# A one-core hybrid decoder step in fp32: cache copies cut batch by batch, side sums and products on other engines, and some tiles at other addresses

## The chip, the cores and the metric

The kernel runs on one core of a Trainium2 chip. The time is device microseconds (us) of one launch, the median of the runs made. Five engines of the core work side by side, each through its own queue of instructions in order: PE (TensorE, matrix products), DVE (VectorE), ACT (ScalarE), POOL (GpSimd) and SP, which here issues DMA transfers only. ACT and POOL issue DMA transfers too.

## The reference

One layer of a decoder, run for a prompt of 1024 tokens and for 8 samples of 8 new tokens, together 1088 tokens of width 1024 (all fp32):

```python
x = x + 0.5 * swiglu(rmsnorm(x, ffn1_norm), ffn1_w_gu, ffn1_w_down)     # hidden width 2816
z = rmsnorm(x, mix_norm) @ w_in                                         # q, k, v, LRU, memory, gates
y_att = attend(q, k, v)            # 3 groups of 4 heads, windows 128, 512, 2048, dilations 1, 4, 16
y_rec = gelu(yr) * rglru(causal_conv(xr))                               # a gated recurrence
y_mem = memory_attention(qm)
x = x + (sigmoid(ga) * (y_att @ w_att_o) + sigmoid(gb) * (y_rec @ w_rec_o)
         + sigmoid(gc) * (y_mem @ w_mem_o)) @ w_out
x = x + 0.5 * swiglu(rmsnorm(x, ffn2_norm), ffn2_w_gu, ffn2_w_down)
y = rmsnorm(x, final_norm)
```

The samples read their keys and values from window caches (`cache_win_k0` to `cache_win_v2`: 8 samples, 128, 512 and 2048 rows of 256 floats), and the caches shifted by 8 rows are outputs of their own (`s_win_k0` to `s_win_v2`). Most of such an output is a plain copy from DRAM to DRAM.

## The kernel before, in words

**Stages.** Everything is held transposed (features in partitions, tokens along the free dimension). The stages follow each other: gate_up1 (the gate and up products of the first FFN, until about 590 us of the profile), down1 (its down product), the mixing part (memory heads, attention heads, then the recurrence in six tiles `lru_tile(0)` to `lru_tile(5)`, with 24 gate tiles strewn in where PE would wait), merge and out_proj, gate_up2 (from about 2030 us), down2 (from about 2530 us) and the final norm.

**One product is three.** `mac3` (L262 to L264) makes an fp32 product of a high and a low part of each operand, as three matmuls. The weights arrive in `wr` tiles by SP's DMAs; ACT rounds them to the high part (L167) and DVE subtracts for the low part (L168); these are the `ws` tiles.

**gate_up.** The hidden width is worked off in 22 pieces p of 128. The tokens lie in two halves tp of 544, and each half in two blocks of 272. The first PLAIN = 3 pieces are plain products (`plain`, L475). The others are "quads": `OPS` lists 7 products of Strassen's scheme in place of 8, whose weight operands are sums of weights, made by `combined` (L172 to L183) on POOL and DVE, and whose data operands `xo` are sums of blocks of x, made by `operands_of_blocks`, `norms_of_blocks` (squares by ACT, sums by L413), `gain_blocks` (L425 on POOL or DVE, L429 on ACT) and `sums_of_blocks` (L437, on DVE, with `put` at L373/L374). What is begun at the start of a stage as a generator (`begin1`, `begin2`) advances one step per `tick()`, and `tick()` is called between products. The last ALONE = 2 pieces are done for one half and then for the other, so that the down product's operand can be loaded meanwhile.

The evacuation (`swiglu`, L528 to L562) gathers the products of a quad in PSUM into `sl` and `uu`: DVE at L538 and L553, ACT at L543, POOL at L556 and L560 (the multiplication by the row factors `rb`). `gated_hidden` (L493) then has ACT's silu (L502), POOL's product (L505) and a DMA store from `sl` to the DRAM buffer `h_d` (L508), which is issued from ACT's queue. `sl` has three buffers: DVE writes a buffer again (L553) once its store has landed. The store's step in ticks is the tuple handed to `gated_hidden`.

**Cache copies.** `cache_copies` (L1545) makes a list of pieces, and `copies(n)` (L1560) issues the next n by DMAs in POOL's queue (L1563). gate_up1 calls `copies(1)` with each p but two, 20 times, gate_up2 `copies(2)` with each until none is left, and `copies(100)` stands at its end.

**The end of gate_up.** When the first half of the ALONE pieces is issued, `change()` closes pools and begins to load the hidden values back (`hr`, `hidden` at L565). In the kernel before, a loop ahead of it ticks until nothing is late.

**down.** `down_tile` (L641) sums the products over k in PSUM; the first sum goes to `x` by an ACT copy (L647), the later ones are added by DVE (L649). In down1 and down2 the squares of the finished x are summed on POOL or DVE (`sumsq`, L313 to L321), then `rstd` (L290 to L299) makes the factors, by a transposition on PE and a power on POOL.

**The sample attention.** `sample_scores` (L950) runs as a side job, a step every second tick: a DMA of a broadcast query into `qb` (L964), the product with the keys (L979, 48 in all: 24 on POOL, 24 on DVE) and the sum over features on DVE (L969). A step totals the product before, issues a load, and multiplies.

PE, ACT, DVE and POOL run in the order in which the code is written; SP's order is the framework's.

Of the kernel before, what the change touches and what calls it, by code (L numbers as in the profile page):

```python
# [53 lines left out]

FILL = (5, 4, 2)

# [4 lines left out]
class Kernel:  # L61
    def __init__(self, ctx, tc, ins, cst, outs):
        self.ctx, self.tc, self.nc = ctx, tc, tc.nc
        self.i, self.c, self.o = ins, cst, dict(zip(_OUTS, outs))
        self.n = 0
        self.ticks = 0
        self.first, self.side, self.due, self.hurry = [], [], [], False
        self.late = 0
        self.raws, self.ready, self.using, self.rest = [], [], 0, iter(())
# [47 lines left out]
    def make_plan(self):  # L117
        i = self.i
        col = lambda name, j: (name, i[name][j], 1024)

        def flat(name, off, n):
            return (name, i[name][off:off + 128 * n].rearrange("(p n) -> p n", p=128), n)

        def ffn(gu, dn):
            plan, off = [], 0
            for n, p in enumerate(TILES):
                plan += [(gu if n < PLAIN else "*" + gu, i[gu][q], 1024) for q in (p, KF + p)]
            for k, nk, w in DOWN:
                n = D if w == D else nk * w
                plan += [flat(dn, off + j * 128 * n, n) for j in range(nk * D // n)]  # L130
                off += 128 * nk * D
            return plan

        gates = [col("w_in", 34 + f) for f in range(24)]
        take = lambda n: [gates.pop(0) for _ in range(min(n, len(gates)))]
        mix = take(3) + [col("w_mem_kv", j) for j in range(8)] + [col("w_in", 30 + h) for h in range(4)]
        mix += take(FILL[0])
        for g, hp in UNITS:
            mix += [col("w_in", base + g * 2 + hp) for base in (12, 6, 0)]
        mix += take(FILL[1])  # L140
        for r in range(KR):
            mix += [col("w_in", 18 + r), col("w_in", 24 + r)] + take(FILL[2] - (r < 2))
        mix += take(24)
        merge = [("w_merge", i["w_merge"][f, u], 768) for f in range(KD) for u in range(2)] * 2
        outp = [col("w_out", f) for f in range(KD)] * 2
        self.plan = ffn("w_gu1", "w_dn1") + mix + merge + outp + ffn("w_gu2", "w_dn2")
# [59 lines left out]
    def make(self):  # L206

        for _ in self.rest:
            return
        if self.raws or self.plan:  # L210
            name, raw, n = self.raw()
# [96 lines left out]

    def norm_chunk(self, c, sq, wait):
        t0, n = CH[c]  # L310
        r = self.rstd(n, sq)
        self.later(wait, lambda: self.rows(self.rbc[:, t0:t0 + n], r, n))
# [119 lines left out]
    def sums_of_blocks(self, tp, xs, eng, rest=lambda: True):  # L432
# [7 lines left out]
        less(b22, b22, b11)  # L440
        yield
        self.put(tp, 6, b22)
        yield
# [10 lines left out]
    def plain(self, gu, p, order, pool):  # L454
# [3 lines left out]
        for tp in order:  # L458
            xo = self.xo[tp]
            sl, uu = (pool.tile([128, 2, TC], F32, name=self.uid(x), tag=x, bufs=n) for x, n in (("sl", 3), ("uu", 3)))  # L460
            for j, ms in enumerate(((1, 2), (0, 3))):
# [11 lines left out]
                def evac(j=j, rb=rb, both=both, sl=sl, uu=uu, tp=tp):  # L473
                    for t, ps in zip((sl, uu), both):
                        nc.vector.tensor_tensor(out=t[:, j], in0=ps[:, :TC], in1=rb, op=OP.mult)  # L475
                    if j:
                        self.gated_hidden(p, tp, sl, uu, (1, 2, 3))
                self.held.append(((tp, j), evac))
# [49 lines left out]
    def swiglu(self, p, tp, pool):  # L528
# [11 lines left out]
        def step(m, ps):  # L540
# [16 lines left out]
            if m == 3:  # L557
                sl = t["sl"]
                plus(sl[:, 1], ps, t["mu"])
                nc.gpsimd.tensor_tensor(out=sl[:, 1], in0=sl[:, 1], in1=rb[:, 1], op=OP.mult)  # L560
                self.gated_hidden(p, tp, sl, t["uu"])
        return step  # L562
# [26 lines left out]
    def gate_up(self, gu, first, pool, copies, misc, change):  # L589
# [15 lines left out]
        for tp in (first, second):  # L605
            for p in range(KF - ALONE, KF):
                self.quad(gu, p, (tp,), pool)
            if tp == first:
                while self.late:
                    self.tick()  # L610
                change()
# [336 lines left out]
    def sample_scores(self, g):  # L948
# [25 lines left out]
        for n in range(16):  # L974
# [3 lines left out]
            kk = kt[n][:, 0:1, :].to_broadcast([128, 4, 256]) if g == 0 else kt[n]  # L978
            (nc.vector if n % 2 else nc.gpsimd).tensor_tensor(out=prev, in0=prev, in1=kk, op=OP.mult)  # L979
            yield  # L980
# [565 lines left out]
    def cache_copies(self):  # L1546
        pieces = []
        for g, (W, _) in enumerate(GROUPS):
            for x in "kv":
                src, dst = (ap.rearrange("b w f -> b (w f)") for ap in (self.i[f"cache_{x}{g}"], self.o[f"s{x}{g}"]))  # L1550
                n = (W - 8) * 256
                nb, cut = ((8, 1), (2, 1), (1, 2))[g]
                for b in range(0, NB, nb):
# [12 lines left out]
def emit(K):  # L1566
# [9 lines left out]
    K.banks(ps0, "psum0", mm=8)  # L1576
    K.xo, K.plained, K.hurry, K.known, K.held = ({}, {}), False, True, set(), []
    of0, stage1 = left(low, "of0"), left(mid, "stage1")
# [30 lines left out]
    ops = [K.operands_of_blocks(tp, xs[tp], g, order) for tp in range(2)]  # L1609
    norms = [K.norms_of_blocks(tp, xs[tp], ev, eng) for tp, eng in enumerate((nc.vector, nc.gpsimd))]  # L1610
    for _ in range(2):
# [6 lines left out]
    def begin1():  # L1618
# [4 lines left out]
        yield from ops[1]  # L1623
        yield from norms[1]
        for _ in zip(K.gain_blocks(xs[0], g, nc.scalar), K.gain_blocks(xs[1], g, nc.gpsimd)):
            yield
        yield from K.sums_of_blocks(0, xs[0], nc.vector)
        spare.close()
# [35 lines left out]
    with ExitStack() as es:  # L1664
        K.tmps = right(es, "tmps1", 2)
        acc = {}

# [3 lines left out]
        def part(c, o):  # L1671
# [5 lines left out]
            K.split_x(c, o, xa, K.v["mix_norm"])  # L1677
            K.sumsq(o, xa, acc[c], n)
            if o % 4 == 3:
                nc.sync.dma_start(K.x_d[0][:, o - 3:o + 1, t0:t0 + n], K.x[:, o - 3:o + 1, t0:t0 + n])  # L1680
            if o == KD - 1:
                K.later(6 if c < 2 else 2, lambda: K.norm_chunk(c, acc[c], 5 if c < 2 else 2))
        K.down("w_dn1", pool, K.raw_tiles(pool), after)
# [12 lines left out]
    with ExitStack() as mix:  # L1696
# [42 lines left out]
        with ExitStack() as es:  # L1739
# [4 lines left out]
            for i in range(KR):  # L1744
                K.lru_tile(i)
                gate(FILL[2] - (i < 2))
            while K.due:
# [9 lines left out]
    K.banks(ps0, "psum5", mm=8)  # L1757
    K.xo, K.plained, K.known, K.held = ({}, {}), False, set(), []
    ev, of1, bb1, stage0 = left(low, "ev2"), left(low, "of1b"), left(low, "bb1"), left(low, "stage0b")
# [19 lines left out]
    def begin2():  # L1779
        yield from K.operands_of_blocks(0, xs[0], g, order, store(0))  # L1780
        yield from K.norms_of_blocks(0, xs[0], ev, nc.vector)
        for _ in zip(K.gain_blocks(xs[1], g, nc.scalar), K.gain_blocks(xs[0], g, nc.gpsimd)):
            yield
        yield from K.sums_of_blocks(1, xs[1], nc.vector)
        spare.close()
# [3 lines left out]
    def ready():  # L1789
        K.hurry = True  # L1790
        K.first += [K.operands_of_blocks(1, xs[1], g, order, store(1)), K.norms_of_blocks(1, xs[1], ev, nc.gpsimd)]
    K.out_proj(xs, ev, ready)
# [16 lines left out]
    with ExitStack() as es:  # L1809
        K.banks(es, "psum6", mm=6, t=2)  # L1810
        pool, K.tmps = left(es, "ffn2"), left(es, "tmps4", 2)
        K.x = pool.tile([128, KD, NT], F32, name="x2")
        acc = {}

# [5 lines left out]
        def square2(c, o):  # L1820
            t0, n = CH[c]
            xa = K.x[:, o, t0:t0 + n]
            if o < KD - 1 or c < 2:
                K.sumsq(o, xa, acc[c], n, nc.vector if c == 2 and o % 2 else None)
            else:
                last = K.tmp("ta")[:, :n]
                nc.scalar.activation(last, xa, AF.Square)
                r = K.rstd(n, acc[c], last)
            if c == 2:
# [6 lines left out]
        def after2(c, o):  # L1836
# [7 lines left out]
            if o == KD - 1:  # L1844
                K.later(5, lambda: K.norm_chunk(c, acc[c], 3))
                for j in range(4):
# [105 lines left out]
```

## Time and profile before

| | |
|---|---|
| median of 3 runs | 2820.39 us (2819.96 to 2821.05) |
| the profiled execution | 2824.31 us, its span 2822.5 us |
| PE busy | 2680.3 us (95%) |
| DVE busy | 1755.2 us (62%) |
| ACT busy | 910.8 us (32%) |
| POOL busy | 808.7 us (29%) |
| mean clock of PE | 0.977 of full |
| moved by DMA | 374.99 MB, 133 GB/s |

PE is nearly always at work, so the time is PE's work, plus the stretches in which PE waits, plus what it loses where the clock granted to it is below 1. A profile row such as "PE pg L262 <- DVE sl L553: 27.6, 5, 8.5" says that PE's instructions of line 262 that write `pg` waited in total 27.6 us, 5 times and 8.5 us at most, and that DVE's instruction of line 553 came last of what they waited for. A chain row such as "143.02 16.14 DMA h_d<-sl" says that from 143.02 us on the chain of work passes for 16.14 us through the store of `sl` to `h_d`.

### The profile page before, as it was taken

To read this page: it belongs to the slowest core of one execution; us is meant where nothing else is said; L and a number is where in the kernel's file an instruction comes from. 1 tells how busy PE (TensorE), PEld (TensorE's weight loads), DVE (VectorE), ACT (ScalarE), POOL (GpSimd) and SP (SyncE) were. 2 spreads that over 40 slices of the span, in tenths; PEclk is the share of its full clock that TensorE was granted. 3 is DMA by queue.
4 is the path that set the end of the run, shared out by engine and by line. 5 is a ranking of instruction groups with operands and counts; after the bars stand their busy time and mean duration, and the time that the engine had idled before them with its cause. 6 is when DMAs were issued, how large, how long until landed. Compare 5 with 4: busy or idle time off the path is not lost.

```text
span 2822.5 us, 46271 instructions
## 1 busy us (share of the span) xinstructions
PE 2680.3 (95%) x18076; PEld 2595.5 (92%) x18076; DVE 1755.2 (62%) x3018; ACT 910.8 (32%) x1747; POOL 808.7 (29%) x745
## 2 busy tenths in 40 slices
PE   7887899999999999999998999999999999989997
PEld 7887799999999889989987899999999999979997
DVE  5654656777785443466677656674567656576766
ACT  6321223321134322323334354432443223242112
POOL 3334455510021000021143321131235455453003
PEclk9998899999999999999999999999999999999998
DMA  4222334342225152375454431855426422243221
GB/s 166 92 88 97 115 130 151 137 173 92 93 96 187 65 163 87 117 242 163 145 183 144 154 114 66 278 173 185 167 102 226 171 105 83 73 138 120 90 78 64
DMA packets 181629, 374.99 MB, mean 133 GB/s; under 512 B 22345, under 2 KB 116745, under 8 KB 180737
## 3 DMA queue, kind: packets, MB, share of 16 engines
q1 hardware_dynamic: 166464, 303.85, 32.6%
q0 software_dynamic: 2272, 43.65, 4.3%
q10 hardware_dynamic: 12672, 24.52, 2.3%
q8 instruction: 142, 2.33, 0.3%
q14 instruction: 79, 0.64, 0.1%
HBM read 305.59 MB, written 113.16 MB: 148 GB/s over the span
## 4 chain that ended last, share of the span: by engine, by line
PE 73%; DVE 8%; DMA 7%; POOL 5%; issue 3%; ACT 3%; SPq 0%; DVEq 0%; ACTq 0%; POOLq 0%
PE pg L262 7%; PE pg L264 7%; PE pg L263 7%; PE z L262 7%; PE z L263 6%; PE z L264 6%; PE pd L262 6%; PE pd L263 6%; PE pd L264 6%; DMA h_d<-sl 4%; DVE ws L168 2%; PE po L264 2%; PE po L263 2%; PE po L262 2%; PE o L815 1%
## 5 line engine op out<-in xcount | busy, mean ns | idle before, releaser
L262 PE MATMUL pg<-xo,ws 128*128 128x272 f32 x2512 | 738.3, 294 | 72.1 <-DVE sl L553 27.6
L263 PE MATMUL pg<-xo,ws 128*128 128x272 f32 x2512 | 733.3, 292 | 0.0
L264 PE MATMUL pg<-xo,ws 128*128 128x272 f32 x2512 | 733.1, 292 | 0.1
L167 ACT ACTIVATE ws<-wr 128x512 fp32r<-128x512 f32 (+1 forms) x550 | 325.4, 613 | 914.7 <-PE pd L264 357.6
L168 DVE TENSOR_TENSOR ws<-wr,ws 128x512 fp32r<-128x512 f32 (+1 forms) x550 | 465.0, 869 | 151.8 <-ACT ws L167 151.4
L262 PEld LDWEIGHTS pg<-xo,ws 128*128 128x128 f32 x2512 | 483.0, 192 | 77.8 <-DVE sl L553 28.6
L262 PE MATMUL z<-xg,ws 128*128 128x368 f32 (+1 forms) x1392 | 478.1, 343 | 6.2 <-DVE ta L1394 6.2
L264 PEld LDWEIGHTS pg<-xo,ws 128*128 128x128 f32 x2512 | 483.1, 192 | 0.9 <-DVE ws L168 0.9
L263 PEld LDWEIGHTS pg<-xo,ws 128*128 128x128 f32 x2512 | 483.3, 192 | 0.0
L264 PE MATMUL z<-xg,ws 128*128 128x368 f32 (+1 forms) x1392 | 459.2, 330 | 0.0
L263 PE MATMUL z<-xg,ws 128*128 128x368 f32 (+1 forms) x1392 | 459.1, 330 | 0.0
L262 PE MATMUL pd<-h,ws 128*128 128x368 f32 (+1 forms) x1056 | 348.6, 330 | 10.4 <-ACT x L647 8.1
L263 PE MATMUL pd<-h,ws 128*128 128x368 f32 (+1 forms) x1056 | 346.5, 328 | 0.0
L264 PE MATMUL pd<-h,ws 128*128 128x368 f32 (+1 forms) x1056 | 345.9, 328 | 0.0
L649 DVE TENSOR_TENSOR x<-x,pd 128x368 f32<-128x368 f32 (+1 forms) x504 | 257.7, 529 | 134.4 <-PE pd L264 134.3
L262 PEld LDWEIGHTS z<-xg,ws 128*128 128x128 f32 x1392 | 264.3, 190 | 22.4 <-issue 13.1
L263 PEld LDWEIGHTS z<-xg,ws 128*128 128x128 f32 x1392 | 264.7, 190 | 1.3
L264 PEld LDWEIGHTS z<-xg,ws 128*128 128x128 f32 x1392 | 263.7, 189 | 0.0
L262 PEld LDWEIGHTS pd<-h,ws 128*128 128x128 f32 x1056 | 199.3, 189 | 11.3 <-ACT x L647 8.4
L263 PEld LDWEIGHTS pd<-h,ws 128*128 128x128 f32 x1056 | 199.4, 189 | 0.0
L264 PEld LDWEIGHTS pd<-h,ws 128*128 128x128 f32 x1056 | 199.3, 189 | 0.0
L183 POOL TENSOR_TENSOR wr<-wr,s 128x512 f32<-128x512 f32 x42 | 56.8, 1353 | 377.4 <-DVE ws L168 377.4
(295 smaller groups left out, 3745.2 us busy)
## 6 DMA issues: line engine op xcount, KB each, us to landing
wr<-in_w_gu_dram SPq DMA_DIRECT2D x96, 512.0 KB
wr<-in_w_in_dram SPq DMA_DIRECT2D x58, 512.0 KB
qb<-qs_d SPq DMA_DIRECT2D x48, 512.0 KB
h_d<-sl ACTq DMA_DIRECT2D x88, 272.0 KB
hr<-h_d SPq DMA_DIRECT2D x44, 544.0 KB
wr<-in_w_dn_dram SPq DMA_DIRECT2D x44, 512.0 KB
out_sk_dram<-in_cache_k_dram POOLq DMA_DIRECT2D x16, 1020.0 KB, 5.7
out_sv_dram<-in_cache_v_dram POOLq DMA_DIRECT2D x16, 1020.0 KB, 7.9
```

The source lines that it names most:

```text
L167: nc.scalar.activation(spl[:, 0, :n], src, AF.Copy)
L168: nc.vector.tensor_tensor(out=spl[:, 1, :n], in0=src, in1=spl[:, 0, :n].bitcast(F32), op=OP.subtract)
L183: eng.tensor_tensor(out=out, in0=x, in1=y, op=op)
L262: nc.tensor.matmul(out, wh, xh, start=start and i == 0, stop=False, **more)
L263: nc.tensor.matmul(out, wh, xl, start=False, stop=False, **more)
L264: nc.tensor.matmul(out, wl, xh, start=False, stop=i == n - 1, **more)
L649: nc.vector.tensor_tensor(out=xa, in0=xa, in1=ps[:, :n], op=OP.add)
L815: nc.tensor.matmul(po[:, e], pt[:, h, j * 128:(j + 1) * 128], z["vt"][:, kb[j], e], start=j == 0, stop=j == len(kb) - 1)
```

## The change

1. `cache_copies`: the pieces are cut from one sample each, with 16 rows as the outermost dimension (`nb = 1`), 1 piece a sample for group 0 (120 KB), 1 for group 1 (504 KB), 2 for group 2 (1020 KB). That makes 64 pieces in place of 42 (2 of 960 KB for group 0, 8 of 1008 KB for group 1, 32 of 1020 KB for group 2). The calls of `copies` are as before.
2. `FILL`: one gate tile more between the attention heads and the recurrence, one fewer after the third recurrence tile.
3. `make()` makes no combined weights before the norms of both halves are done (`normed`). The norms' additions of the second half are on DVE in place of POOL in both FFNs; the gains change places between ACT and POOL, and one of them runs beside the norms. `sums_of_blocks` has one step more.
4. `gated_hidden` of the plain pieces and of the ALONE pieces runs at other ticks; L560 of the ALONE pieces is on DVE; the loop ahead of `change()` is gone.
5. All 48 products of `sample_scores` are on POOL.
6. The last chunk of tokens in down1 and down2 has its sums of squares in two tiles, even o on POOL in the one and odd o on DVE in the other, which `rstd` adds up (in down1 all of them were on POOL in one tile; in down2 they alternated into one tile).
7. `x` of down2 stands in a pool of its own behind `tmps4` and `ffn2`, so that its address is another one.

```diff
-FILL = (5, 4, 2)
+FILL = (5, 5, (1, 1, 1, 2, 2, 2))
...
-            mix += [col("w_in", 18 + r), col("w_in", 24 + r)] + take(FILL[2] - (r < 2))
+            mix += [col("w_in", 18 + r), col("w_in", 24 + r)] + take(FILL[2][r])
...
-        if self.raws or self.plan:
+        if (self.raws or self.plan) and (self.normed or (self.raws or self.plan)[0][0][0] != "*"):
...
-    def norm_chunk(self, c, sq, wait):
+    def norm_chunk(self, c, wait, *sq):
         t0, n = CH[c]
-        r = self.rstd(n, sq)
+        r = self.rstd(n, *sq)
...
         less(b22, b22, b11)
         yield
+        yield
         self.put(tp, 6, b22)
...
-                        self.gated_hidden(p, tp, sl, uu, (1, 2, 3))
+                        self.gated_hidden(p, tp, sl, uu, (2, 3, 4))
...
-                nc.gpsimd.tensor_tensor(out=sl[:, 1], in0=sl[:, 1], in1=rb[:, 1], op=OP.mult)
-                self.gated_hidden(p, tp, sl, t["uu"])
+                (nc.gpsimd if p < KF - ALONE else nc.vector).tensor_tensor(out=sl[:, 1], in0=sl[:, 1], in1=rb[:, 1], op=OP.mult)
+                self.gated_hidden(p, tp, sl, t["uu"], (4, 5, 7) if p < KF - ALONE else (1, 3, 4))
...
             if tp == first:
-                while self.late:
-                    self.tick()
                 change()
...
-            (nc.vector if n % 2 else nc.gpsimd).tensor_tensor(out=prev, in0=prev, in1=kk, op=OP.mult)
+            nc.gpsimd.tensor_tensor(out=prev, in0=prev, in1=kk, op=OP.mult)
...
-                nb, cut = ((8, 1), (2, 1), (1, 2))[g]
+                nb, cut = 1, (1, 1, 2)[g]
...
-    norms = [K.norms_of_blocks(tp, xs[tp], ev, eng) for tp, eng in enumerate((nc.vector, nc.gpsimd))]
+    norms = [K.norms_of_blocks(tp, xs[tp], ev, eng) for tp, eng in enumerate((nc.vector, nc.vector))]
...
-        yield from norms[1]
-        for _ in zip(K.gain_blocks(xs[0], g, nc.scalar), K.gain_blocks(xs[1], g, nc.gpsimd)):
-            yield
+        for _ in zip(norms[1], K.gain_blocks(xs[0], g, nc.gpsimd)):
+            yield
+        K.normed = True
+        yield from K.gain_blocks(xs[1], g, nc.scalar)
...
-            K.sumsq(o, xa, acc[c], n)
+            if c == 2 and o % 2:
+                K.sumsq(o // 2, xa, odd, n, nc.vector)
+            else:
+                K.sumsq(o, xa, acc[c], n)
...
-        yield from K.norms_of_blocks(0, xs[0], ev, nc.vector)
-        for _ in zip(K.gain_blocks(xs[1], g, nc.scalar), K.gain_blocks(xs[0], g, nc.gpsimd)):
-            yield
+        for _ in zip(K.norms_of_blocks(0, xs[0], ev, nc.vector), K.gain_blocks(xs[1], g, nc.gpsimd)):
+            yield
+        K.normed = True
+        yield from K.gain_blocks(xs[0], g, nc.scalar)
...
-        K.first += [K.operands_of_blocks(1, xs[1], g, order, store(1)), K.norms_of_blocks(1, xs[1], ev, nc.gpsimd)]
+        K.first += [K.operands_of_blocks(1, xs[1], g, order, store(1)), K.norms_of_blocks(1, xs[1], ev, nc.vector)]
...
-        pool, K.tmps = left(es, "ffn2"), left(es, "tmps4", 2)
-        K.x = pool.tile([128, KD, NT], F32, name="x2")
-        acc = {}
+        K.tmps, pool, rest = left(es, "tmps4", 2), left(es, "ffn2"), left(es, "x2")
+        K.x = rest.tile([128, KD, NT], F32, name="x2")
+        acc, odd = {}, pool.tile([128, CMAX], F32, name="odd2", tag="odd", bufs=1)[:, :CH[2][1]]
...
-                K.sumsq(o, xa, acc[c], n, nc.vector if c == 2 and o % 2 else None)
+                if c == 2 and o % 2:
+                    K.sumsq(o // 2, xa, odd, n, nc.vector)
+                else:
+                    K.sumsq(o, xa, acc[c], n)
             else:
...
-                r = K.rstd(n, acc[c], last)
+                r = K.rstd(n, acc[c], odd, last)
```

**POOL's queue in gate_up1, around the first quad.** `wr` at L183 are combined weights, `uu` and `sl` the evacuation of the quad; the copies are L1563 before and L1562 after. Before:

```order
L1563 DMA out_sk_dram<-in_cache_k_dram 2x8x16128
L183 TENSOR_TENSOR wr_620<-wr_620,s_891 128x512
L183 TENSOR_TENSOR wr_900<-wr_898,wr_900 128x512
L183 TENSOR_TENSOR wr_898<-wr_898,s_1181 128x512
L556 TENSOR_TENSOR uu_1223<-uu_1223,rbc 128x544
```

And after:

```order
L1562 DMA out_sk_dram<-in_cache_k_dram 16x1920
L183 TENSOR_TENSOR wr_620<-wr_620,s_890 128x512
L183 TENSOR_TENSOR wr_899<-wr_897,wr_899 128x512
L183 TENSOR_TENSOR wr_897<-wr_897,s_1181 128x512
L557 TENSOR_TENSOR uu_1223<-uu_1223,rbc 128x544
```

The copy stands at the same place of the row; its shape was two outer rows of 8 by 16128 floats, and is 16 rows of 1920 floats.

**POOL's queue at the end of gate_up2.** The last two quads of the ALONE pieces, then the first residual additions of down2 (`x`, `xr`). Before:

```order
L556 TENSOR_TENSOR uu_25074<-uu_25074,rbc 128x544
L560 TENSOR_TENSOR sl_25111<-sl_25111,rbc 128x272
L505 TENSOR_TENSOR sl_25111<-sl_25111,uu_25074 128x544
L556 TENSOR_TENSOR uu_25206<-uu_25206,rbc 128x544
L560 TENSOR_TENSOR sl_25247<-sl_25247,rbc 128x272
L505 TENSOR_TENSOR sl_25247<-sl_25247,uu_25206 128x544
L1818 TENSOR_TENSOR x_25307<-x_25307,xr_25549 128x1088
```

And after:

```order
L557 TENSOR_TENSOR uu_25093<-uu_25093,rbc 128x544
L506 TENSOR_TENSOR sl_25131<-sl_25131,uu_25093 128x544
L557 TENSOR_TENSOR uu_25228<-uu_25228,rbc 128x544
L506 TENSOR_TENSOR sl_25268<-sl_25268,uu_25228 128x544
L1562 DMA out_sv_dram<-in_cache_v_dram 16x16320 x4
L1822 TENSOR_TENSOR x_25334<-x_25334,xr_25577 128x1088
```

The multiplication of `sl` by the row factors has left POOL, and four copies of 1020 KB have come in behind the last hidden product.

**DVE's queue where the recurrence begins.** `sst` totals a product of the sample attention, `qb` is the product itself, `xe` and `xc` are the convolution of the first recurrence tile. Before:

```order
L1322 SCALAR_TENSOR_TENSOR xc_13889<-xe_13888,vec,xc_13889 128x392 x3
L969 TENSOR_REDUCE sst_13518<-qb_13939 128x4x4
L979 TENSOR_TENSOR qb_13975<-qb_13975,kv_13937 128x1024
L168 TENSOR_TENSOR ws_14040<-wr_13598,ws_14040 128x512
L168 TENSOR_TENSOR ws_14043<-wr_13772,ws_14043 128x512
```

And after:

```order
L1321 SCALAR_TENSOR_TENSOR xc_14005<-xe_14004,vec,xc_14005 128x392 x3
L968 TENSOR_REDUCE sst_13520<-qb_14053 128x4x4
L168 TENSOR_TENSOR ws_14154<-wr_13774,ws_14154 128x512
L168 TENSOR_TENSOR ws_14157<-wr_13893,ws_14157 128x512
L1367 TENSOR_TENSOR lY_14009<-z_14141,rbc 128x352
```

DVE's product is gone from between the total and the next weight parts.

More of the change, by code (lines that the diff above doesn't have):

```diff
@@ L67, in __init__ @@
         self.first, self.side, self.due, self.hurry = [], [], [], False
-        self.late = 0
+        self.late, self.normed = 0, False
         self.raws, self.ready, self.using, self.rest = [], [], 0, iter(())
@@ L1576, in emit @@
     K.banks(ps0, "psum0", mm=8)
-    K.xo, K.plained, K.hurry, K.known, K.held = ({}, {}), False, True, set(), []
+    K.xo, K.plained, K.hurry, K.known, K.held, K.normed = ({}, {}), False, True, set(), [], False
     of0, stage1 = left(low, "of0"), left(mid, "stage1")
@@ L1665, in emit @@
         K.tmps = right(es, "tmps1", 2)
-        acc = {}
+        acc, odd = {}, K.tmps.tile([128, CMAX], F32, name="odd1", tag="odd", bufs=1)[:, :CH[2][1]]
         def after(c, o):
@@ L1681, in part @@
             if o == KD - 1:
-                K.later(6 if c < 2 else 2, lambda: K.norm_chunk(c, acc[c], 5 if c < 2 else 2))
+                K.later(6 if c < 2 else 2, lambda: K.norm_chunk(c, 5 if c < 2 else 2, acc[c], *([odd] if c == 2 else [])))
         K.down("w_dn1", pool, K.raw_tiles(pool), after)
@@ L1745, in emit @@
                 K.lru_tile(i)
-                gate(FILL[2] - (i < 2))
+                gate(FILL[2][i])
             while K.due:
@@ L1757, in emit @@
     K.banks(ps0, "psum5", mm=8)
-    K.xo, K.plained, K.known, K.held = ({}, {}), False, set(), []
+    K.xo, K.plained, K.known, K.held, K.normed = ({}, {}), False, set(), [], False
     ev, of1, bb1, stage0 = left(low, "ev2"), left(low, "of1b"), left(low, "bb1"), left(low, "stage0b")
@@ L1810, in emit @@
         K.banks(es, "psum6", mm=6, t=2)
-        pool, K.tmps = left(es, "ffn2"), left(es, "tmps4", 2)
-        K.x = pool.tile([128, KD, NT], F32, name="x2")
-        acc = {}
+        K.tmps, pool, rest = left(es, "tmps4", 2), left(es, "ffn2"), left(es, "x2")
+        K.x = rest.tile([128, KD, NT], F32, name="x2")
+        acc, odd = {}, pool.tile([128, CMAX], F32, name="odd2", tag="odd", bufs=1)[:, :CH[2][1]]
         def residual(o):
@@ L1844, in after2 @@
             if o == KD - 1:
-                K.later(5, lambda: K.norm_chunk(c, acc[c], 3))
+                K.later(5, lambda: K.norm_chunk(c, 3, acc[c]))
                 for j in range(4):
```

## The prediction

> **What bounds the kernel now.** I read the busy times first, then the stretches, then in each stretch who waited for whom. The page says that PE works 2680.3 us of the span, so the end is set by PE's work, by the holes in it and by the clock granted to it.
>
> ```profile
> PE 2680.3 (95%) x18076; PEld 2595.5 (92%) x18076; DVE 1755.2 (62%) x3018; ACT 910.8 (32%) x1747; POOL 808.7 (29%) x745
> ```
>
> The stretches below (columns: from and to, length, busy time and count of each engine, mean clock, DMA share, GB/s) are those with holes, but for the third, which has none.
>
> ```profile
> 0.00:113.00 113.00, 89.25 (x636) 87.61 (x637) 66.28 (x120) 54.85 (x111) 36.86 (x36) 0.92 0.34 128
> 113.00:327.00 214.00, 170.74 (x1239) 166.64 (x1238) 116.51 (x161) 50.30 (x88) 89.69 (x92) 0.90 0.27 96
> 327.00:548.00 221.00, 221.00 (x1750) 218.84 (x1750) 146.93 (x230) 67.60 (x120) 120.69 (x97) 1.00 0.40 138
> 548.00:592.00 44.00, 34.67 (x239) 33.06 (x238) 32.07 (x49) 17.62 (x29) 19.27 (x13) 0.96 0.76 288
> 840.00:862.00 22.00, 17.01 (x99) 16.16 (x98) 16.73 (x36) 12.85 (x26) 15.38 (x14) 0.92 0.49 158
> 1425.00:1525.00 100.00, 84.69 (x465) 78.45 (x464) 77.26 (x123) 43.71 (x59) 41.96 (x47) 0.91 0.47 147
> 2025.00:2100.00 75.00, 70.06 (x519) 69.04 (x519) 56.95 (x93) 38.97 (x76) 25.89 (x21) 0.95 0.46 163
> 2480.00:2545.00 65.00, 51.81 (x356) 50.48 (x354) 42.69 (x58) 26.35 (x47) 28.26 (x19) 0.89 0.39 133
> ```
>
> Two losses stand in such a row: length minus PE's busy time is the hole, and one minus the clock, times the length, is about what PE lost by running slower behind it. Row two has 43.3 us of holes and a clock of 0.90: by far the worst place, though it does the work of row three.
>
> **The copies (the largest term).** Between 113 and 327 us PE and DVE wait as follows, and the chain passes through the store of the hidden values once for each quad, six times, of which the first and the last:
>
> ```profile
> PE pg L262 <- DVE sl L553: 27.6, 5, 8.5
> ...
> DVE sl L553 <- DMA h_d<-sl: 85.4, 6, 16.3
> ...
> 143.02 16.14 DMA h_d<-sl
> ...
> 297.68 20.76 DMA h_d<-sl
> ```
>
> A store of 272 KB takes 16 to 21 us, DVE can't write `sl` again until then, and PE waits for DVE to empty PSUM. What lies in front of the stores is seen in the issues of the same stretch (count, KB each, median us to landing):
>
> ```profile
> out_sv_dram<-in_cache_v_dram POOLq DMA_DIRECT2D x4, 1008.0 KB, 24.0
> ...
> out_sk_dram<-in_cache_k_dram POOLq DMA_DIRECT2D x3, 1008.0 KB, 22.6
> ...
> out_sk_dram<-in_cache_k_dram POOLq DMA_DIRECT2D x1, 1020.0 KB, 5.3
> ```
>
> Nearly the same bytes land in 24.0 or 5.3 us, so it is the shape that decides: the slow pieces have 2 as their outermost dimension, the fast one 16, and while a slow one runs the stores land late. After the change every piece has 16 rows. In the third stretch there is such a piece of 16 rows for each p,
>
> ```profile
> out_sk_dram<-in_cache_k_dram POOLq DMA_DIRECT2D x10, 1020.0 KB, 5.3
> ```
>
> and PE has no hole at all.
>
> The price: row three does 1750 matmuls in 221 us, 0.1263 us each. The 1239 of row two would take 156.5 us at that pace instead of 214, so 57.5 us go. The bounds are 64.7 us (43.3 of holes and 0.10 × 214 = 21.4 of clock) and, if other waits come forward, about 45. I take **−57**.
>
> The Trainium skill, page "DMA: Bandwidth & Descriptors", section "Why a DMA increments its semaphore by 16 and not by 1", says that a transfer uses the largest number up to 16 of engines that divides its slowest dimension. By that rule the old pieces have 2 engines, the new ones 16, and the store is freed; the trace agrees in so far as 24.0 stands against 5.3 us.
>
> The rest of the copies moves: gate_up1 issues 16 pieces of 120 KB and 4 of 504 KB, gate_up2 two pieces with all of 20 p's in place of 11, and the last four (4.2 MB) go out at its end. In the first part of gate_up2, with two 1020-KB pieces for each p, the row is:
>
> ```profile
> 2100.00:2260.00 160.00, 160.00 (x1281) 159.96 (x1280) 99.46 (x157) 46.51 (x81) 78.12 (x67) 1.00 0.51 179
> ```
>
> No hole, clock 1.00, so I take nothing for the added p's. The four at the end meet the first loads of down2: by 4 × 5.3 us at most 21 us of queueing, covered by what down2 has already in its tiles; I take 0, the range has +5.
>
> **The end of gate_up2 (2480 to 2545).** Holes 13.2 us, clock 0.11 × 65 = 7.2 us.
>
> ```profile
> PE pd L262 <- ACT x L647: 8.1, 1, 8.1
> PE pg L262 <- DVE uu L538: 3.9, 2, 3.0
> ...
> ACT sl L502 <- POOL sl L560: 9.7, 2, 5.1
> ...
> ACT x L647 <- DMA h_d<-sl: 6.2, 1, 6.2
> ...
> 2530.76 7.08 DMA h_d<-sl
> ```
>
> The first copy to `x` waits for a store, since x2 lies where `sl` lay; with its own pool that wait is gone (the last row is the chain's: it goes through the store for 7.1 of PE's 8.1 us). What is late next is ACT's silu and POOL's product ahead of the store, which were through at 2530.76 us, about when PE began to wait; with L560 on DVE the silu, which waits for POOL in the third row, comes earlier. The removed loop took the 3.9 us with it: ACT, POOL and DVE were brought to a halt there. Of 20.4 us I take **−14**; ends −20 and −8 (the wait for `x` alone), since the load of `hr` still waits for the last stores.
>
> **The start (0 to 113).**
>
> ```profile
> PE pg L262 <- ACT ws L167: 19.1, 2, 11.6
> PE t L306 <- POOL rs L299: 2.9, 2, 2.3
> ...
> L413 POOL TENSOR_TENSOR acc<-acc,sq 128x272 f32<-128x272 f32 x14 | 10.7, 769 | 0.9
> ```
>
> The 11.6 us are the first load and stay. Of the 12.2 us of holes left and 9 of clock, POOL's additions (14 × 0.769 = 10.7 us) and the wait that follows go to DVE, and the first copy shrinks from 960 to 120 KB. DVE gets those 14 and keeps its long subtractions; the combined weights must wait for the norms, which can starve the first quads. **−7**; ends −14 and +3.
>
> **The end of gate_up1 (548 to 592).** The same loop and the same silu: holes 9.3, clock 1.8 us.
>
> ```profile
> PE pg L262 <- DVE uu L538: 6.5, 4, 3.1
> ...
> 566.77 10.60 DMA hr<-h_d
> ```
>
> The load of `hr` behind x's loads is untouched. **−4**; ends −11 and +2.
>
> **The end of down1.** POOL's chain of sums of the last chunk is halved by DVE's other tile. The row of 840 to 862 has 5.0 us of holes, of which
>
> ```profile
> PE t L294 <- POOL acc L321: 4.2, 1, 4.2
> ```
>
> DVE has 5.3 us free there. **−4** of 6.8 with the clock; ends −7 and −1.
>
> **The sample products.** A product is 1.217 us on DVE, 2.397 on POOL:
>
> ```profile
> L979 POOL TENSOR_TENSOR qb<-qb,kv x24: 2361/2397/2859, 1180.2 to 1482.6; 128x1024 f32<-128x1024 f32 x24
> L979 DVE TENSOR_TENSOR qb<-qb,kv x24: 1214/1217/1490, 1185.7 to 1491.7; 128x1024 f32<-128x1024 f32 x24
> ```
>
> DVE is freed of 24 × 1.217 = 29.2 us and POOL gets 57.5. Near 1246 us DVE stood at such a product, waiting for its load, with the attention's work queued behind it:
>
> ```profile
> DVE qb L979 <- DMA qb<-qs_d: 4.7, 1, 4.7
> ...
> PE s L786 <- DVE s L789: 1.7, 1, 1.7
> PE o L815 <- ACT pt L805: 1.1, 1, 1.1
> ```
>
> Now POOL waits there, and behind it stands little: **−3** (the two waits of PE, 2.8; ends −6 with the clock, and +2).
>
> At the start of the recurrence (1425 to 1525) DVE works 77 of 100 us, and PE waits:
>
> ```profile
> PE g L1333 <- issue: 7.5, 1, 7.5
> PE z L262 <- DVE ta L1394: 6.2, 2, 4.5
> ```
>
> There lie 15.3 us of holes and 9 of clock. Five products (6.1 us) leave DVE, and the gate tile that now comes ahead lets some steps of the side job end before the recurrence. Against it, in order of time, DVE's row of the chain without and with a product of POOL beside it, and that product:
>
> ```profile
> 1442.60 0.61 DVE xc L1322
> ...
> 1446.11 2.62 DVE xc L1322
> ...
> 1445.74 2.56 POOL L979 TENSOR_TENSOR qb<-qb,kv 128x1024 f32<-128x1024 f32 x1 [9.24 <-DMA qb<-qs_d]
> ```
>
> The convolution step took 0.61 us, and 2.62 where POOL's product ran from 1445.74 on: it ended 0.4 us after that did (1448.73 against 1448.30). I take **−6**, what leaves DVE; ends −16 and +19 (the rival below).
>
> The Trainium skill, page "SBUF — State Buffer", section "Who interferes with whom", says that a DVE instruction with two SBUF inputs and a GpSimd one that reads SBUF exclude each other for the whole instruction, so this part is bought dearer than it looks. The trace agrees: 2.62 against 0.61 us. By the rule alone, each of 24 products could hold DVE for up to 2.4 us, an estimate that would turn the −6 into a loss.
>
> **Merge to gate_up2 (2025 to 2100).** The same moves as at the start: holes 4.9, clock 3.8 us. **−3**; ends −8 and +5. The last norm's tiles I cost at nothing: their additions alternate between engines either way.
>
> **The sum.** −57 −14 −7 −4 −4 −3 −6 −3 = −98 us. From the profiled execution's 2824.31 us that is 2726.3; the median of the runs, 2820.39, lies 3.9 lower, so the forecast is **2722 us**.
>
> **Rivals.**
>
> *The products cost what they free (12%).* Each of the 24 moved products delays a DVE instruction by 2.62 − 0.61 = 2.0 us: 48 us against 29.2 freed, 19 us more for DVE in a part where it is nearly full. If all falls on PE, the −6 becomes +19: 2722 + 25 = 2747 us. For it speaks the row at 1446.11; against it, that half the products ran on POOL already and PE stood still for less than 3 us near 1246.
>
> *Only the stall of the stores goes (8%).* What else is moved comes out even: 2820.4 − 57 = 2763 us. For it, that DVE takes on additions where it is busy; against it, that the wait of `x` for a store is an address alone.
>
> *The change doesn't free the stores (5%).* They are as late behind pieces of 16 rows, or something else holds them: 2820.4 − 41 = 2779 us. Row three speaks against it.
>
> *Slower: bytes, not shape, delay the stores (2%).* Seven pieces in row two cost 57.5 us, 8.2 each. gate_up2 gets 18 more pieces; if each cost as much there, 148 us would be added: 2722 + 148 = 2870 us. It ends above the time before from 98 / 18 = 5.4 us a piece on. Against it: 160 us without a hole at two pieces a p.
>
> **Chances and range.** The forecast has 72%, its own range 2698 to 2745: the ends of the terms won't all fall together, so some 24 us to either side. With the products' rival and the one of the stall alone, 92% lie between 2698 and 2763; that is the range. About 0.2% (5.6 us) is what a measurement of this kernel can tell from no change: faster by more 97%, within it 1%, slower by more 2%.
>
> **What would show it.** Right: between 113 and 327 us no wait of DVE's L553 for `h_d`, quads of one pace through gate_up1, a clock near 1.00; no wait of ACT's first `x` copy for `h_d`; fewer than 10 us of holes around the end of gate_up2. Wrong: stores that land after 15 us in either gate_up (the copies); PE waiting for weights in the first quads (the start); longer waits of PE for DVE in 1180 to 1525 us, with the two-input rows of DVE stretched (the products); `hr` or weights late at the start of down2 (the four last copies). The forecast fails if gate_up1 loses less than 45 us.

## The result, and the profile after

The changed kernel takes 2746.96 us (median of 4 runs, 2746.11 to 2749.58) against 2820.18 us of the kernel before on the same chip: ratio 0.9743, 95% interval 0.9726 to 0.976, so about 73 us faster, where 98 were forecast. The profiled execution after took 2746.11 us (span 2744.3), and 78.2 us lie between it and the profiled one of before, which was itself 4 us above its median.

The stretches of the kernel after that answer to those of before (columns as there):

```profile
113.00:327.00 214.00, 214.00 (x1699) 212.08 (x1698) 133.83 (x226) 66.08 (x115) 119.29 (x119) 1.00 0.29 95
...
485.00:516.00 31.00, 25.80 (x188) 24.93 (x187) 27.35 (x39) 14.60 (x23) 12.06 (x8) 0.94 0.85 332
772.00:794.00 22.00, 17.86 (x104) 16.93 (x104) 17.56 (x39) 12.63 (x26) 10.39 (x10) 0.92 0.47 153
...
1380.00:1500.00 120.00, 104.62 (x606) 93.97 (x605) 94.31 (x180) 52.82 (x75) 55.52 (x66) 0.93 0.48 148
...
2420.00:2465.00 45.00, 39.87 (x288) 38.48 (x287) 36.50 (x51) 23.08 (x42) 20.68 (x15) 1.00 0.49 170
```

Between 113 and 327 us the holes are gone, the clock is full, and no wait of DVE's L554 for `h_d` is left. The end of gate_up1 (485 to 516), the end of down1 (772 to 794) and above all the start of the recurrence (1380 to 1500) still have holes. Who PE waits for in the last of these and at 1194 us, and how long the copies take to land in gate_up1:

```profile
PE t L1020 <- ACT ss L1012: 8.3, 1, 8.3
PE s L785 <- DVE s L788: 5.4, 1, 5.4
PE g L1332 <- DVE xc L1321: 3.5, 1, 3.5
...
out_sk_dram<-in_cache_k_dram POOLq DMA_DIRECT2D x4, 504.0 KB, 3.8
out_sk_dram<-in_cache_k_dram POOLq DMA_DIRECT2D x8, 120.0 KB, 3.2
```

Two waits for DVE and one for the sample softmax (behind DVE's L1011) are new in this size. The matrix products that bound the stages, read from the two traces (by their starts; the last product of down1 by its end), give the account of the time:

| stage | before, us | after, us | gain | forecast |
|---|---|---|---|---|
| gate_up1, until the first product of down1 | 582.9 | 515.7 | 67.2 | 68 (copies 57, start 7, end 4) |
| down1, until the end of its last product | 265.2 | 264.4 | 0.9 | 4 |
| mixing, until the last product of `z` | 944.5 | 947.6 | -3.1 | 9 (3 and 6) |
| merge, out_proj, until the first product of gate_up2 | 244.6 | 241.4 | 3.2 | 3 |
| gate_up2, until the first product of down2 | 486.9 | 484.3 | 2.6 | 14, with down2 |
| down2, until its last product | 276.3 | 269.4 | 6.9 | (see above) |

The row of the changed kernel's down products has the first boundary and, to 0.4 us, the last:

```profile
L262 PE MATMUL pd<-h,ws x1056: 317/330/508, 515.7 to 2722.4; 128*128 128x352 f32 x166, 128*128 128x368 f32 x10
```

So gate_up1 gained what was forecast, and the mixing part, which should have gained, lost. The loss is larger than this pair of traces shows: two kernels below whose mixing part is the one of before took 940.4 and 941.2 us for it (b_copies_new, b_g1_last). The experiments ask three things: was it the shape of the copies; what did the products on POOL cost; and what held the end of gate_up2 free.

### The profile page after: what moved, and what is told of

Same layout as the page of the kernel before. It is cut to its first block, busy times and chain, and to the rows that moved or that the text cites. A ratio compares the mean times of both kernels' runs of the same rounds, so it can differ in the third digit from the quotient of the medians.

```text
span 2744.3 us, 46291 instructions
## 1 busy us (share of the span) xinstructions
PE 2658.8 (97%) x18088; PEld 2578.8 (94%) x18088; DVE 1728.8 (63%) x3032; ACT 910.3 (33%) x1747; POOL 834.4 (30%) x751
## 3 DMA queue, kind: packets, MB, share of 16 engines
q1 hardware_dynamic: 166464, 303.85, 33.7%
## 4 chain that ended last, share of the span: by engine, by line
PE 83%; DVE 10%; ACT 2%; issue 2%; DMA 2%; POOL 1%; SPq 0%; DVEq 0%; ACTq 0%; POOLq 0%
PE pg L262 9%; PE pg L264 9%; PE pg L263 9%; PE z L262 7%; PE z L263 7%; PE z L264 7%; PE pd L262 6%; PE pd L263 6%; PE pd L264 6%; DVE ws L168 2%; PE po L264 2%; PE po L263 2%; PE po L262 2%; PE o L814 1%; PE wo L262 1%
## 5 line engine op out<-in xcount | busy, mean ns | idle before, releaser
L168 DVE TENSOR_TENSOR ws<-wr,ws 128x512 fp32r<-128x512 f32 (+1 forms) x550 | 439.4, 822 | 133.7 <-ACT ws L167 133.3
L262 PEld LDWEIGHTS pg<-xo,ws 128*128 128x128 f32 x2512 | 476.5, 190 | 21.3 <-DVE uu L539 12.8
L264 PEld LDWEIGHTS pg<-xo,ws 128*128 128x128 f32 x2512 | 476.4, 190 | 5.8 <-DVE ws L168 5.8
L263 PEld LDWEIGHTS pg<-xo,ws 128*128 128x128 f32 x2512 | 476.8, 190 | 0.0
L262 PEld LDWEIGHTS z<-xg,ws 128*128 128x128 f32 x1392 | 265.2, 191 | 15.7 <-issue 14.2
L978 POOL TENSOR_TENSOR qb<-qb,kv 128x1024 f32<-128x1024 f32 x48 | 116.2, 2424 | 198.0 <-DMA qb<-qs_d 146.6
```

Source lines behind the costliest of these rows:

```text
L168: nc.vector.tensor_tensor(out=spl[:, 1, :n], in0=src, in1=spl[:, 0, :n].bitcast(F32), op=OP.subtract)
L262: nc.tensor.matmul(out, wh, xh, start=start and i == 0, stop=False, **more)
L263: nc.tensor.matmul(out, wh, xl, start=False, stop=False, **more)
L264: nc.tensor.matmul(out, wl, xh, start=False, stop=i == n - 1, **more)
L978: nc.gpsimd.tensor_tensor(out=prev, in0=prev, in1=kk, op=OP.mult)
```

## The experiments

Ratios are to the kernel before on the same chip, with their 95% intervals; the medians of before there were 2822.8, 2821.4 and 2823.3 us in three groups of runs. A difference to the changed kernel is the difference of ratios times 2821 us. In traces of kernels whose gate_up1 is alike it ends between 514.6 and 519.3 us, so a difference of less than 5 us between two traces is not read there.

| kernel | median, us | ratio, interval | against the changed kernel |
|---|---|---|---|
| changed kernel | 2746.96 | 0.9743 (0.9726 to 0.976) | |
| a_copies_old | 2804.25 | 0.9933 (0.9919 to 0.9946) | +54 us |
| b_copies_new | 2774.57 | 0.9831 (0.9818 to 0.9845) | (48 us under before) |
| b_g1_last | 2800.15 | 0.9929 (0.9916 to 0.9943) | (20 us under before) |
| a_x2_old | 2768.78 | 0.9813 (0.9798 to 0.9829) | +20 us |
| a_flush | 2753.77 | 0.9759 (0.9745 to 0.9774) | +4.5 us |
| a_alternate | 2742.94 | 0.972 (0.9707 to 0.9734) | -6.5 us |
| a_dve_all | 2736.47 | 0.9697 (0.9684 to 0.9711) | -13 us |
| a_read | 2747.50 | 0.9738 (0.9722 to 0.9755) | -1.4 us |
| a_write | 2739.22 | 0.9708 (0.9692 to 0.9725) | -10 us |
| a_total_late | 2750.02 | 0.9749 (0.9731 to 0.9766) | +1.7 us |
| a_fill_old | 2747.84 | 0.9738 (0.9725 to 0.9752) | -1.4 us |
| a_dve_fill | 2736.39 | 0.97 (0.9683 to 0.9718) | -12 us |

**Was it the shape of the copies?** First the old pieces in the changed kernel:

```diff
-                nb, cut = 1, (1, 1, 2)[g]
+                nb, cut = ((8, 1), (2, 1), (1, 2))[g]
```

> The changed kernel with the cache copies cut as before (2, 8 and 32 pieces). Shape theory: pieces with 2 as outermost dimension hold up the stores of the hidden values, so the waits of DVE's L554 for h_d come back in the first third of gate_up1 and the time rises by 55 to 62 us, to about 2805 us. Rival, the stores were late for another reason that other parts of the change removed: less than 20 us, below 2767 us.

It takes 2804.25 us, 54 more, and DVE waits again as in the kernel before (between 113 and 327 us):

```profile
DVE sl L554 <- DMA h_d<-sl: 81.8, 6, 16.0
```

So the stall is the copies'. Then the new pieces alone in the kernel before (the same two lines the other way round):

> The kernel before with only the cache copies cut batch by batch. Shape theory: the whole stall goes, 55 to 60 us, to about 2763 us, and DVE's L553 doesn't wait for h_d between 113 and 327 us. Rival, that the copies need the other parts to pay: under 40 us, above 2780 us.

2774.57 us: 48 us, not 57, and short of what was expected. gate_up1 has them all: it ends at 519.5 us, 63.4 earlier than before, and PE works without a hole again:

```profile
113.00:327.00 214.00, 214.00 (x1697) 212.08 (x1697) 137.97 (x227) 66.94 (x117) 121.47 (x120) 1.00 0.28 96
```

But at the start of down2 the same kernel has (PE's wait, ACT's wait, and the chain between 2455 and 2490 us):

```profile
PE pd L262 <- ACT x L647: 18.9, 1, 18.9
...
ACT x L647 <- DMA h_d<-sl: 16.9, 1, 16.9
...
2465.76 17.83 DMA h_d<-sl
```

In the kernel before the same store took 7.08 us and PE's wait was 8.1. The four copies that now go out at the end of gate_up2 lie in front of it, and these 4.2 MB, issued within 2 us, land after 8.0 to 16.2 us although each has 16 rows. So the copies give some 11 us of their gain back there, as long as `x` lies where `sl` lay.

The last of this group keeps the pieces and the bytes of before and changes their order only, in the kernel before:

```diff
-        return pieces
+        return pieces[:2] + pieces[10:] + pieces[2:10]
```

> The kernel before with its own 42 pieces, only in another order: the eight pieces of 1008 KB (2 outer rows) last, the 32 of 1020 KB (16 rows) ahead of them, so that gate_up1 moves as many bytes as before. Shape theory: the stall leaves gate_up1 whole (some 57 us) and comes up in gate_up2 where the eight are issued, two by two in four p's, with some 20 to 40 us lost there: 2785 to 2805 us. Rival, that the bytes of a copy decide: gate_up1 stalls as before, and the time stays within 10 us of 2820 us.

2800.15 us, as the shape theory has it. Its gate_up1 and a part of gate_up2, what landed in each (the first row in gate_up1, the second in gate_up2), and the chain in gate_up2, first and last of four:

```profile
113.00:327.00 214.00, 214.00 (x1698) 212.08 (x1697) 137.40 (x225) 67.28 (x117) 118.71 (x120) 1.00 0.40 140
2100.00:2260.00 160.00, 137.64 (x1040) 136.12 (x1038) 84.81 (x119) 36.68 (x66) 66.33 (x57) 0.93 0.37 137
...
out_sk_dram<-in_cache_k_dram POOLq DMA_DIRECT2D x16, 1020.0 KB, 5.4
...
out_sk_dram<-in_cache_k_dram POOLq DMA_DIRECT2D x4, 1008.0 KB, 23.2
...
2147.64 19.47 DMA h_d<-sl
...
2242.61 19.52 DMA h_d<-sl
```

gate_up1 moves the same megabyte with each p as before (140 GB/s against 96) and has no hole; the stall has moved to gate_up2, to the four p's that issue the pieces of two outer rows, with a store of 19.5 us each. gate_up1 ends 57 us earlier than before (525.5 us), and gate_up2 takes 36 more (523.0 against 486.9). For this stall the bytes are no cause, the shape is.

**What held the end of gate_up2 free?** `x` of down2 back at its old place, the rest as changed:

```diff
-        K.tmps, pool, rest = left(es, "tmps4", 2), left(es, "ffn2"), left(es, "x2")
-        K.x = rest.tile([128, KD, NT], F32, name="x2")
+        pool, K.tmps = left(es, "ffn2"), left(es, "tmps4", 2)
+        K.x = pool.tile([128, KD, NT], F32, name="x2")
```

> The changed kernel with x of down2 back in the pool with ffn2, ahead of tmps4, where sl lay. Theory that the address keeps the end of gate_up2 free, and more so now that four copies go out there: ACT's first copy to x waits for the last stores again, behind 4 MB of copies, PE stands still 15 to 20 us at the start of down2 and loses some 8 us of clock behind it: 2768 to 2775 us. Rival, that other edits of the end (L560 on DVE, other ticks) already free it: within 5 us of 2747 us.

2768.78 us, 20 more, at the lower end of what was expected. It has the wait of the kernel with the new copies alone:

```profile
PE pd L262 <- ACT x L646: 18.3, 1, 18.3
...
ACT x L646 <- DMA h_d<-sl: 17.1, 1, 17.1
```

Then the loop ahead of `change()`:

```diff
             if tp == first:
+                while self.late:
+                    self.tick()
                 change()
```

> The changed kernel with the loop that ticks until nothing is late ahead of change again. Theory that the removed loop was worth what its waits showed, some 4 us in each FFN: 5 to 10 us slower, about 2754 us. Rival, that the waits of PE for DVE's L539 come from the order of the single quads and not from the loop: within 3 us of 2747 us.

2753.77 us: 4.5 us by the ratios, whose intervals overlap, where 5 to 10 were expected. PE's waits at the end of gate_up1 (480 to 525 us), with the loop and, in the second row, in the changed kernel without it:

```profile
PE pg L262 <- DVE uu L539: 7.1, 3, 3.0
```

```profile
PE pg L262 <- DVE uu L539: 6.6, 5, 3.1
```

They are nearly the same, so the waits that the forecast charged to the loop belong to the order of the single quads, as the rival said. Something does go with the loop, but little: gate_up2 takes 486.6 us with it, and 483.1 to 484.4 in the kernels that have the changed one's gate_up2.

**What did the products cost?** Alternating again, and all on DVE:

```diff
-            nc.gpsimd.tensor_tensor(out=prev, in0=prev, in1=kk, op=OP.mult)
+            (nc.vector if n % 2 else nc.gpsimd).tensor_tensor(out=prev, in0=prev, in1=kk, op=OP.mult)   # a_alternate
+            nc.vector.tensor_tensor(out=prev, in0=prev, in1=kk, op=OP.mult)                             # a_dve_all
```

> The changed kernel with the sample products alternating between POOL and DVE again. Theory that the all-POOL products cost the mixing part what was forecast as gain (DVE's total L968 now waits for POOL's product, 34 us in all): 6 to 14 us faster, about 2737 us, and the waits of L968 for POOL mostly gone. Rival, that the gate tile moved ahead of the recurrence or the attention's own order is what costs: within 3 us of 2747 us.

> The changed kernel with all 48 sample products on DVE. If the wait of the total for POOL's slow product is the cost, the load's latency stays and DVE waits at the product instead: about 2747 us, no better than alternating. If the cost is that POOL's product blocks DVE's two-input instructions, none is blocked now: faster than the alternating version, below 2737 us. If DVE's own load decides, 29 us more of DVE work over the alternating version: slower than 2750 us.

Alternating is 6.5 us faster by the ratios, but the intervals overlap, and its profiled execution, the slowest of its four, isn't faster; the waits of L968 for POOL's product fall to 3.7 us in it. All on DVE is 13 us faster, clear of the interval: the fastest version but for one that equals it. The groups of DVE between 1100 and 1440 us, in the changed kernel (total of a product, low parts of the weights, convolution):

```profile
L968 DVE TENSOR_REDUCE sst<-qb 128x16 f32<-128x1024 f32 x48 | 58.3, 1215 | 33.7 <-POOL qb L978 33.7
L168 DVE TENSOR_TENSOR ws<-wr,ws 128x512 fp32r<-128x512 f32 x40 | 32.9, 863 | 1.3 <-ACT ws L167 1.2
L1321 DVE SCALAR_TENSOR_TENSOR xc<-xe,vec,xc 128x352 f32<-128x352 f32 (+2 forms) x10 | 10.0, 1000 | 0.4
```

And with all products on DVE:

```profile
L978 DVE TENSOR_TENSOR qb<-qb,kv 128x1024 f32<-128x1024 f32 x48 | 59.3, 1236 | 11.4 <-DMA qb<-qs_d 11.0
L968 DVE TENSOR_REDUCE sst<-qb 128x16 f32<-128x1024 f32 x48 | 58.1, 1211 | 0.0
L168 DVE TENSOR_TENSOR ws<-wr,ws 128x512 fp32r<-128x512 f32 x40 | 25.7, 683 | 1.0 <-ACT ws L167 0.9
L1321 DVE SCALAR_TENSOR_TENSOR xc<-xe,vec,xc 128x352 f32<-128x352 f32 (+2 forms) x18 | 10.9, 604 | 0.6
```

Two things differ: DVE's total waits 33.7 us for POOL's product, and the instructions with two inputs take longer beside it (L168 863 ns against 683, L1321 1000 against 604; the total, with one input, is the same). Three kernels are to tell the two apart. In the first all products are on DVE and POOL does an idle product beside each, whose result nobody waits for; in the second POOL does fills in its place, which write only (in both a copy of one column makes POOL wait for DVE's product, and the keys have two buffers in place of three):

```diff
+            nc.gpsimd.tensor_copy(scr[:, 0, 0:1], prev[:, 0, 0:1])                          # both
+            nc.gpsimd.tensor_tensor(out=scr, in0=scr, in1=prev, op=OP.mult)                 # a_read
+            for _ in range(3):                                                              # a_write
+                nc.gpsimd.memset(scr, 0.0)
```

> The changed kernel with all sample products on DVE, and beside each of them a product of the same size on POOL that reads the query tile and a scratch tile and whose result nobody uses or waits for (the keys have two buffers in place of three, to make room). Theory that POOL's reading blocks DVE's two-input instructions: the 10 us that all-DVE won are lost again, 2744 to 2752 us, and the mean of L168 between 1100 and 1440 us rises from 0.68 to about 0.86 us. Rival, that the wait of the total for POOL's slow product was the cost: within 4 us of 2737 us, L168 at 0.7 us.

> The same with three fills of the scratch tile on POOL in place of the idle product, about as long, which write and don't read. If reading is what blocks: within 4 us of 2737 us, L168 near 0.7 us. If any work on POOL there delays (its own queue, or writing too): 2744 us or more.

```profile
L168 DVE TENSOR_TENSOR ws<-wr,ws 128x512 fp32r<-128x512 f32 x40 | 30.5, 804 | 0.2
...
L982 POOL TENSOR_TENSOR scr<-scr,qb 128x1024 f32<-128x1024 f32 x48 | 121.5, 2531 | 3.8
```

```profile
L168 DVE TENSOR_TENSOR ws<-wr,ws 128x512 fp32r<-128x512 f32 x40 | 25.7, 683 | 0.9 <-ACT ws L167 0.8
...
L983 POOL MEMSET scr<- 128x1024 f32 x144 | 137.5, 955 | 8.4
```

With the idle product (the first fence) the time is 2747.50 us, as slow as the changed kernel, and L168 takes 804 ns; with more POOL time spent in fills (the second) it is 2739.22 us and L168 takes 683 ns, as with POOL free. The load of the next query does have to wait until the idle product has read the tile, but that is not the cause: DVE waits 9.9 us in all for these loads in a_read, 8.5 in a_write and 11.0 in a_dve_all. The difference lies in the mixing part (bounds as in the table of the stages):

| | changed kernel | a_alternate | a_dve_all | a_read | a_write | a_total_late |
|---|---|---|---|---|---|---|
| mixing, us | 947.6 | 946.6 | 936.8 | 946.7 | 940.0 | 951.0 |

PE's wait for the convolution in a_read, and a step of it in the chain, which took 0.46 to 0.48 us with POOL free and ends here 0.2 us after POOL's idle product does:

```profile
PE g L1336 <- DVE xc L1325: 5.7, 3, 2.0
...
1388.01 2.54 DVE xc L1322
```

The third kernel leaves the products on POOL and totals each one step later, so that DVE should wait less:

```diff
-            if n:
-                total(n - 1, prev)
-            prev, cur = cur, fetch(n + 1)
+            if n > 1:
+                total(n - 2, two)
+            two, prev, cur = prev, cur, fetch(n + 1)
```

> The changed kernel, all products on POOL, with the total of a product one step later (three query tiles, two key tiles), so that DVE need not wait for a product that has just begun. Wait theory: the 34 us of waits of L968 shrink to a few and the time falls to about 2737 us. Theory that POOL's reading blocks DVE: the waits shrink too, but the time stays within 4 us of 2747 us, L168 at 0.86 us.

```profile
L968 DVE TENSOR_REDUCE sst<-qb 128x16 f32<-128x1024 f32 x48 | 58.0, 1212 | 11.1 <-POOL qb L978 11.1
L168 DVE TENSOR_TENSOR ws<-wr,ws 128x512 fp32r<-128x512 f32 x40 | 37.9, 986 | 7.1 <-ACT ws L167 7.0
```

The waits of the total fall from 33.7 to 11.1 us and the time doesn't: 2750.02 us. But this does not part the two causes. L168 rises from 863 to 986 ns meanwhile, and one of the waits that are left, of 7.7 us, lies in PE's way. In the changed kernel too the hole at 1194 us comes by such a wait: DVE's total stands behind a query's load and POOL's product, and the attention's scores (L788) behind the total. The chain there, in the changed kernel, and PE's wait for the scores that is left in a_total_late:

```profile
1187.33 5.20 DMA qb<-qs_d
...
1192.69 2.37 POOL qb L978
...
1196.22 2.59 DVE ws L168 x2
```

```profile
PE s L785 <- DVE s L788: 4.1, 1, 4.1
```

So a_read and a_write show that POOL's reading beside DVE is enough to make the mixing part as slow as in the changed kernel, with no wait for a product. In the changed kernel itself both are at work, and how its loss is shared between them stays open.

**The gate tile.** `FILL` as before, in the changed kernel and in the one with all products on DVE:

```diff
-FILL = (5, 5, (1, 1, 1, 2, 2, 2))
+FILL = (5, 4, (1, 1, 2, 2, 2, 2))
```

> The changed kernel with FILL as before, so that the recurrence begins one gate tile earlier. Theory of the forecast, that the tile ahead lets steps of the side job end before the recurrence: 3 to 8 us slower, about 2752 us. Rival, that the gate tile only moves work and the wait for the sample softmax stands there either way: within 3 us of 2747 us, or faster.

> The changed kernel with all sample products on DVE and FILL as before: the gate tile was worth nothing with POOL's products, so within 4 us of 2737 us. If DVE, fuller now, decides where the recurrence begins, the tile ahead of it is worth some 5 us: about 2742 us.

2747.84 and 2736.39 us: nothing either way. With the old FILL PE stands still where it did in the kernel before (between 1360 and 1500 us), with the new one for the sample softmax (8.3 us in the changed kernel, 8.4 with all products on DVE, so that wait is not the products'):

```profile
PE z L262 <- DVE ta L1393: 6.1, 2, 3.4
PE g L1332 <- issue: 5.5, 1, 5.5
```

## Why the prediction was right, and where its sum was off

The time lies within the range, 25 us above the forecast and 2 us above the forecast's own range (2698 to 2745), to which 72% were given. 5 us of the 25 are the profiled execution of before, which stood 4 us above its median where that of after stands 1 us below. The rest by the steps:

- *The copies*, -57: right in mechanism, and nearly in size. a_copies_old is 54 us slower, and b_g1_last shows that shape alone moves the stall. The rival that bytes decide falls with it. gate_up1 gained 67 of the forecast 68 us, of which the new pieces alone bring 63.4 (b_copies_new), 3.8 of these by the smaller first copy (below): some 60 where 57 were put down. That "the old pieces have 2 engines" fits the eight of 1008 KB only: the two of 960 KB have 8 as outermost dimension, and landed in 8.6 and 7.6 us.
- *The four last copies*, taken at nothing: nearly right in the changed kernel (down2 takes 269.4 us, and 267.4 in a_copies_old, which has none of them there), but only because `x` has its own place. b_copies_new shows the price without it, a hole of 18.9 us in place of 8.1. "Covered by what down2 has already" was not the cover; the address was.
- *The end of gate_up2*, -14: 9.6 measured. The wait of `x` went as the step says, and a_x2_old prices it at 20 us in the kernel as changed, more than was put down, since the copies lie there now. The 3.9 us laid to the loop did not go with it: PE still waits 4.0 us for DVE's L539 between 2420 and 2465 us.
- *The start and the end of gate_up1*, -7 and -4: some 8 us in place of 11, a difference within the scatter. The step held that the 11.6 us of the first load stay; they don't, and that is half of the 8. With a first copy of 120 KB PE waits there as follows, 7.8 us in b_copies_new, and 11.6 again with the old pieces in a_copies_old:

```profile
PE pg L262 <- ACT ws L167: 7.9, 1, 7.9
```

  The other 4 us (519.5 of b_copies_new less 515.7, and 582.9 less the 579.0 of a_copies_old) are the rest of the change there, the norms on DVE among it, and no more than the scatter. At the end the chain still passes through the load of `hr` (7.93 us), as the step says.
- *The end of down1*, -4: 0.9 measured. The step took DVE's free time for cover, 5.3 of 22 us. In the trace after the chain goes on DVE from one instruction to the next (the second tile's sums among them), and PE still waits for a sum:

```profile
781.28 0.45 DVE odd L321
781.73 0.45 DVE x L648
782.17 1.09 DVE xg L282
783.26 0.45 DVE x L648
...
PE t L294 <- POOL acc L321: 2.9, 1, 2.9
```

- *The sample products*, -3 and -6: the steps that failed. The mixing part lost 3.1 us against the trace of before, and 6 to 7 against b_g1_last and b_copies_new, in place of gaining 9. The -3 rested on "behind it stands little": behind POOL's product stands DVE's total, which waited 33.7 us for it, with the attention's scores behind; PE's wait for these was 1.7 us before and is 5.4 now. The -6 took "what leaves DVE" for the value, and left out what the row at 1446.11 showed and the first rival said: the moved products hold DVE up. a_read and a_write show the rival's mechanism; its size was too large (25 us, where all on DVE gives back 13, the waits included). Its time, 2747 us, agrees with the measured one only by the sum of the other misses.
- *The rule of the Trainium skill*, page "SBUF — State Buffer", section "Who interferes with whom", weighed in that step, is borne out in both its halves: a GpSimd instruction that reads SBUF slows DVE's two-input ones (804 to 986 ns against 683), one that only writes doesn't (683). The step had rule and row before it and put too little on them. The rule of the Trainium skill, page "DMA: Bandwidth & Descriptors", section "Why a DMA increments its semaphore by 16 and not by 1", on the number of engines agrees too, 5.4 against 23.2 us for about the same bytes, though no view here counts the engines of one transfer.
- *The gate tile*: part of the -6, worth nothing.

What is shown ends there. How the loss of the mixing part is shared between the waits for POOL's products and their reading, and whether alternating is faster than all on POOL (its runs lie between 2739.0 and 2748.1 us), stays open.

The version to keep is the changed kernel with all 48 products on DVE: 2736.47 us, ratio 0.9697 (0.9684 to 0.9711), faster than the kernel before and than the changed one.

## What to carry to other kernels

Look at the outermost dimension of a long background copy before its size: here one of 2 made stores of another queue land after 16 to 21 us, and the wait showed up far from the copy, as an engine that couldn't write a buffer again. Work moved from DVE to POOL is not free when DVE has work of its own beside it: read the mean duration of DVE's other instructions, not only its busy share, and ask which instruction of DVE waits for the moved one. And price a cover by what it rests on: the same four copies cost some 2 us or some 11 by the address of one tile.

## What the runs showed of the hardware

- Copies of 1008 KB with 2 outer rows landed in 22.4 to 24.4 us wherever they were issued (before, a_copies_old, b_g1_last), ones of 960 KB with 8 in 7.3 to 9.2; ones of 1020 KB with 16 in 5.0 to 11.8 us, and four issued within 2 us at the end of gate_up2 (the changed kernel, b_copies_new, a_x2_old) in 7.1 to 16.8. A store of 272 KB beside the first kind took 16 to 21 us, one behind the four 17.8 us (b_copies_new).
- POOL's product of 128x1024 floats took 2.40 us as its median in the kernel before and 2.41 in a_read, so the delay lies mostly on DVE's side. It is not only instructions with two inputs that are drawn out: of the three steps of L1322 (one input) in a_read between 1100 and 1440 us two took 2.4 and 2.5 us, and one of the changed kernel's four took 2.5, against 0.46 to 0.48 in a_dve_all:

```profile
L1322 DVE TENSOR_SCALAR xc<-xe,vec 128x352 f32<-128x352 f32 (+2 forms) x3 | 5.4, 1795 | 0.3
```

- POOL's fills, 137.5 us of them in 340 us, left DVE's L168 at 683 ns.
